# First mixer of a two-layer decoder trunk: hand-ordered loops replaced by planned strands, with halved products and three partial output sums

## The chip, the cores and the metric

The kernel runs on one core of one Trainium2 chip. The metric is device time in microseconds (us); lower is better. Engines: PE (TensorE: matrix products and transposes), PEld (its weight loads), DVE (VectorE), ACT (ScalarE), POOL (GpSimd), and SP (SyncE, which issues nearly all DMAs).

## What is computed

The reference runs two decoder layers on 256 tokens of width 1024, in float32. Each layer is a half-step feed-forward block, a mixer, and a second half-step feed-forward block, with a normalization before and after each. The change concerns the mixer of the first layer, in which two branches share one input and one output projection:

```
def nsa_ssd_mixer(h, ...):
    proj = h @ w_in
    q, kc, vc, ks, vs, kw, vw, gl, z, xbc, dt = split(proj)
    q, kc, ks, kw = rope(q) / 8, rope(kc), rope(ks), rope(kw)
    o_a = nsa_attention(...)      # per head: gated sum of three softmax attentions over 15
                                  # compressed keys (kc, vc), selected blocks (ks, vs), a window (kw, vw)
    o_b = mamba2_branch(...)      # conv over 4 tokens + silu, chunked state-space scan (2 chunks of 128),
                                  # times silu(z), then an rms norm per group of 512 channels and token
    return concatenate([o_a, o_b], -1) @ w_out
```

The compressed keys and values are `silu(blk @ w1) @ w2`, where `blk` is 32 tokens plus a learned position term `pe`. With 256 tokens every block is selected and the window covers all, so the last two attentions are causal softmaxes over all tokens.

## The kernel before, in words

**Weights.** Weights stream from HBM in units of up to 512 KB. Each unit is split into two float32r parts, `whi` (written by ACT) and `wlo` (the rest, by DVE), and a product with activations, split the same way, is three float32r products (`mm3`, L323). Raw units sit in four buffers (`raw`), split pairs in two rings: `ringa` with 4 pairs, which always exists, and `ringb` with 6, open only in some stages (`ring`, L643).

**Stages.** First feed-forward block (f10), first mixer (`mix0`, L661), second block (f20), third block (f11), second mixer (`mix1`, L1142), last block (f21). `constants` (L607), called inside f10, loads tables. The two token tiles (t = 0, 1, of 128 tokens) share each weight unit; `lagged` (L467) runs t = 1 a few units behind t = 0.

**Order of work.** In the feed-forward blocks and in `mix0` the order on each engine follows the program text, which the framework's scheduler may rearrange. While `strict` is set (`_Engine`, L101), every instruction depends on the one issued before it on its engine, so the text is the order. `mix1` is written as strands: generators that yield the engine they want next and what they wait for. `_Plan` (L145) keeps a time for every engine, prices instructions (`count`, L190), and always advances the strand whose next step can start first, counting its priority in ns as a delay (`run`, L239).

**The mixer now.** `work_a` (L752) computes q, then k and v, then the rest with m0a's 12 units; `qkv_end` (L715) applies the rotation and transposes. Then `ringb` closes and `compress` (L818), `attend_cmp` (L856), `scores` (L884), `values` (L916) and the 12 projections `do_xbc` (L792) run in a loop whose lags are written out by hand; `scores` multiplies all 128 partitions of q by keys with the other head group's rows zeroed (`kTz`), and DVE adds the mask while it takes the maximum (`pr`). Then `ringb` reopens, and a second loop (L1088) runs `decays` (L1026), the 8 gate projections `do_z` (L804), `outputs` (L1053), `gated` (L1061) and `normed` (L1075); the last scales each token by its norm through a product with a diagonal matrix (`dg`). Finally `work_o` (L1109) and `finish` (L573) form the output product with m0o's 12 units, over all 12 in one accumulation per token tile and half, then the norm and the residual. PSUM has four `acc` banks, two `fill` banks (projections, and t = 0 of the output product) and two `tp` banks (transposes).

**The parts that the change touches most.** In `compress` the bias of the hidden layer, `pe` times `w1`, is 16 products of one column per branch, on tiles `pv` and `cwp`; `values` runs all products of one output half (v) before the other's; `decays` multiplies float32 `da`, spread over 128 columns, by a triangular table, and masks the first chunk with one float32r product and the second on DVE.

## Time and profile before

| what | value |
|---|---|
| time before, median of 3 runs | 1214.81 us (1214.44 to 1224.08) |
| the profiled execution's own time | 1214.29 us |
| its span (first to last instruction) | 1212.5 us |
| PE busy | 1183.3 us (98%) |
| DVE busy | 775.7 us (64%) |
| ACT busy | 596.2 us (49%) |
| HBM read | 189.24 MB, 157 GB/s over the span |

Busy time of PE is the union of its matmul records; a record lasts longer than the step from one product to the next, since they are pipelined. The granted clock (PEclk) is given as a share of 2.4 GHz; it has two levels, 1.2 and 2.4 GHz. In this trace nearly every instruction is recorded under the helper's line L112, so groups are told apart by tile names: `fill<-xth,whi` is a product written to a `fill` bank from tiles `xth` and `whi`. A float32 product appears as two instructions, a float32r product as one.

### The profile page before, as it was taken

What the parts mean: (1) busy time and instruction counts of PE and PEld (TensorE: products, weight loads), DVE (VectorE), ACT (ScalarE), POOL (GpSimd) and SP (SyncE); (2) the same over time, 40 slices, a digit from 0 to 9 for tenths busy, and PEclk for the clock granted to TensorE, in tenths of its full rate; (3) what the DMA queues carried; (4) which work ended last, traced back from release to release, by engine and by line L of the source; (5) the groups of instructions that cost most, each with busy time, mean ns of one, the idle gap of its engine ahead of it and who ended that gap; (6) DMA issues with size and microseconds to landing.
All of it is one profiled execution on the core that took longest, in us unless ns stands there. A gap on an engine that the chain in (4) does not pass through costs nothing. (4 is left out here: it accounts for less than half of the span.)

```text
span 1212.5 us, 17861 instructions
## 1 busy us (share of the span) xinstructions
PE 1183.3 (98%) x6888; PEld 999.4 (82%) x6888; DVE 775.7 (64%) x1401; ACT 596.2 (49%) x992; POOL 15.8 (1%) x43
## 2 busy tenths in 40 slices
PE   8999999989999999999999999989999999999997
PEld 6888887878997788888888888889988887888885
DVE  6755548677697765554675564457894688755543
ACT  6655545447663564553465554256234135655531
POOL 0000000000000000000000000001100000000000
PEclk9999999889999999999999999999999999999999
DMA  8765563512163176555575555340414131755540
GB/s 302 248 200 184 189 181 94 202 53 88 49 232 121 55 261 206 191 177 193 169 235 185 188 191 188 116 168 25 154 61 156 39 121 65 264 195 189 189 158 35
DMA packets 53876, 191.46 MB, mean 158 GB/s; under 512 B 6621, under 2 KB 6621, under 8 KB 53662
## 3 DMA queue, kind: packets, MB, share of 16 engines
q1 hardware_dynamic: 53790, 190.31, 46.3%
q8 instruction: 54, 0.88, 0.3%
q14 instruction: 32, 0.26, 0.1%
HBM read 189.24 MB, written 1.05 MB: 157 GB/s over the span
## 5 line engine op out<-in xcount | busy, mean ns | idle before, releaser
L112 DVE SCALAR_TENSOR_TENSOR wlo<-raw,gch,whi 128x1024 fp32r<-128x1024 f32 (+2 forms) x214 | 237.0, 1125 | 143.9 <-ACT whi L112 143.5
L112 ACT ACTIVATE whi<-raw,gch 128x1024 fp32r<-128x1024 f32 (+2 forms) x214 | 214.0, 1023 | 152.7 <-PE acc L112 110.6
L112 DVE TENSOR_TENSOR wlo<-raw,whi 128x1024 fp32r<-128x1024 f32 x120 | 146.5, 1224 | 123.9 <-ACT whi L112 123.9
L112 PE MATMUL acc<-whi,xtl 128*128 128x512 f32 (+1 forms) x576 | 223.6, 388 | 1.1 <-DVE xtl L112 1.1
L112 PE MATMUL acc<-wlo,xth 128*128 128x512 f32 (+1 forms) x576 | 224.1, 390 | 0.0
L112 PE MATMUL acc<-whi,xth 128*128 128x512 f32 (+1 forms) x576 | 221.9, 392 | 0.3 <-DVE u L112 0.3
L112 ACT CAST whi<-raw 128x1024 fp32r<-128x1024 f32 x120 | 125.9, 1051 | 140.5 <-PE acc L112 114.1
L112 PE MATMUL acc<-whi,hth 128*128 128x512 f32 x352 | 137.6, 391 | 0.0
L112 PE MATMUL acc<-whi,htl 128*128 128x512 f32 x352 | 137.1, 389 | 0.0
L112 PE MATMUL acc<-wlo,hth 128*128 128x512 f32 x352 | 137.0, 389 | 0.0
L112 PEld LDWEIGHTS acc<-whi,xtl 128*128 128x128 f32 x576 | 108.3, 188 | 23.2 <-DVE xtl L112 1.5
L112 PEld LDWEIGHTS acc<-whi,xth 128*128 128x128 f32 x576 | 108.8, 189 | 22.0 <-DVE u L112 0.7
L112 PEld LDWEIGHTS acc<-wlo,xth 128*128 128x128 f32 x576 | 108.5, 188 | 20.9
L112 PE MATMUL acc<-whi,xt 128*128 128x512 f32 x352 | 111.0, 391 | 0.0
L112 PEld LDWEIGHTS acc<-whi,htl 128*128 128x128 f32 x352 | 66.1, 188 | 13.9
L112 PEld LDWEIGHTS acc<-whi,hth 128*128 128x128 f32 x352 | 66.1, 188 | 13.6
L112 PEld LDWEIGHTS acc<-wlo,hth 128*128 128x128 f32 x352 | 66.1, 188 | 13.5
L112 PEld LDWEIGHTS acc<-whi,xt 128*128 128x128 f32 x352 | 66.0, 188 | 13.5
L112 PE MATMUL acc<-wlo,xt 128*128 128x512 f32 x176 | 69.0, 392 | 0.0
L112 PE MATMUL fill<-xth,whi 128*128 128x256 f32 x160 | 48.2, 302 | 4.0 <-DVE c L112 3.8
L112 PE MATMUL fill<-xth,wlo 128*128 128x256 f32 x160 | 47.2, 296 | 0.0
L112 PE MATMUL fill<-xtl,whi 128*128 128x256 f32 x160 | 47.2, 295 | 0.0
(380 smaller groups left out, 1695.3 us busy)
## 6 DMA issues: line engine op xcount, KB each, us to landing
raw<-in_wst_dram SPq DMA_DIRECT2D x301, 512.0 KB, 3.5
lw<-in_wst_dram SPq DMA_DIRECT2D x12, 512.0 KB, 3.5
grow<-in_rows_dram SPq DMA_DIRECT2D x9, 512.0 KB, 4.8
wlo<-in_wst_dram SPq DMA_DIRECT2D x8, 512.0 KB, 4.8
whi<-in_wst_dram SPq DMA_DIRECT2D x8, 512.0 KB, 5.0
wr<-in_wst_dram SPq DMA_DIRECT2D x8, 512.0 KB, 11.1
lw<-in_lw_dram SPq DMA_DIRECT2D x3, 512.0 KB, 3.6
raw<-in_wst_dram SPq DMA_DIRECT2D x4, 296.0 KB, 3.1
```

Source lines behind the costliest of these rows:

```text
L112: r = f(out, *a, **k)
```

## The change

`mix0` is rewritten as strands, ordered by `_Plan` with priorities of its own, and emitted with `strict` on. The output of f10's second token tile is normalized inside the mixer (`second`). PSUM has six `acc` banks throughout. k and v are computed before q. The bias of `compress` is computed once in `constants` (`cbias`) from another load of `w1`. The two branches of `compress` alternate between output partitions 0-63 and 64-127, as do the heads in `values` and `outputs`; `scores` uses the 64 partitions of one head group each, without zeroed rows. The causal mask is added by a float32r product of the identity and a mask whose entries are 0 and 1e30 (signs are turned: scores are negated, and their minimum is taken). `decays` uses two float32r parts of `da` and a mask product for both chunks. The output product has three partial sums (attention, and the two groups of the state-space branch); the group's norm weight goes into the output weights (`split`), and the token's norm scales the partial sum (`summed`). `normed` and `dg` are gone. The projections use ring `ringa` with four pairs; `ringb` closes once both `work_a` strands are done, its place holds the mixer's tiles, and it reopens after the last output (`swap`).

```diff
-    a = [(w, 2 * h, 2, c) for c in (qc, kv, rest) for h in range(4)]
+    a = [(w, 2 * h, 2, c) for c in (kv, qc, rest) for h in range(4)]
...
+                ns = max(n / 0.6 + 5, 1.68 * m) * (0.65 if out.shape[0] <= 64 and n >= 30 else 1.0 if a[0].shape[0] > 64 else 0.55 if n > 200 else 0.8)
...
+    PRIORITY0 = {"scale": 500, "normed": 282, "work_a": 300, "end_k": 249, "end_q": -300, "end_r": -389, "split_a": 0, "split":
+                 100, "project": 300, "convolved": 204, "gate": 0, "compress": -366, "attend": 141, "scores":
+                 200, "values": 100, "steps": 213, "products0": 410, "tokens0": 163, "carry": 647, "decays":
+                 -17, "weights": 300, "outputs": 141, "gated": 195, "project_out": 497, "summed": 324,
+                 "finish": 98, "split_f": 330, "second": 200}
...
+            if kind == "mixer":
+                self.y1 = y(1)
+            else:
+                self.postnorm(1, y(1), grow_post, half)
...
+        w = self.xp.tile([P, 2, 16, 64], F32, name="cw", tag="x8")
+        nc.sync.dma_start(w, self.cw[:, 0:2048].rearrange("p (s j e) -> p s j e", s=2, e=64))
+        self.cbias = self.cp.tile([P, 1], F32, name="cbias")
+        tp = self.tpp.tile([P, 4, P], F32, name="tp", tag="tp")
+        for i in range(2):
+            nc.vector.tensor_mul(w[:, i], w[:, i], self.pvt[:, 76 + 16 * i:92 + 16 * i, None].to_broadcast([P, 16, 64]))
+            sums = self.sm.tile([P, 64], F32, name="cbs", tag="cbs", bufs=2)
+            nc.vector.tensor_reduce(sums, w[:, i].rearrange("p j e -> p e j"), axis=mybir.AxisListType.X, op=ALU.add)
+            nc.tensor.matmul(tp[64 * i:64 * i + 64, 0, 0:1], sums, self.tabt[:, 767:768], start=True, stop=True)
+        nc.vector.tensor_scalar(self.cbias, tp[:, 0, 0:1], 0.5, None, op0=ALU.mult)
...
+        def split(name, i, where):
...
+            yield "act", ev("raw", name, i), where, *([ev("ring")] if name == "f20" else [])
+            if where is sl:
+                yield "act", sl
...
+            g = self.gain(ph[name], i) if name in ("m0a", "f20") else normw[:, i - 4:i - 3, None] if name == "m0o" and i > 3 else None
+            if g is None:
+                nc.scalar.copy(hi, x)
+                yield "dve"
+                nc.vector.tensor_sub(lo, x, hi.bitcast(F32))
+            else:
+                for k in range(sh[1]):
+                    if k:
+                        yield "act"
+                    nc.scalar.activation(hi[:, k], x[:, k], AF.Copy, scale=g[:, k])
+                    yield "dve"
+                    nc.vector.scalar_tensor_tensor(lo[:, k], x[:, k], g[:, k], hi[:, k].bitcast(F32), op0=ALU.mult, op1=ALU.subtract)
...
+        def project(name, i):
+            yield "pe", pa, ev(name, i), ev("xn", 0), ev("xn", 1)
+            a = acc((S,))
+            hi, lo = us[name, i]
+            for k in range(KD):
+                self.mm3(a, hi[:, k, :], lo[:, k, :], xn[0][:, k, :], xn[1][:, k, :], k == 0, k == 7)
+                if k % 2 and k < 7:
+                    yield "pe"
+            give(ra)
...
+            ps = acc()
+            R = [slice(64 * i, 64 * i + 64) for i in range(2)]
+            for j in range(16):
+                for i in range(2):
+                    nc.tensor.matmul(ps[R[i], 0:30], w1[i][:, j, :], cst[:, 2 * i:2 * i + 2, 2 * j:2 * j + 225:16], start=j == 0, stop=j == 15)
+                if j % 4 == 3 and j < 15:
+                    yield "pe"
...
+            nc.scalar.activation(ht[:, 0, :], ps[:, 0:30], AF.Tanh, scale=0.5, bias=self.cbias)
+            nc.scalar.activation(ht[:, 1, :], ps[:, 0:30], AF.Identity, scale=0.5, bias=self.cbias)
+            yield "dve"
...
         def scores(t, g):
...
             ns = P * (t + 1)
...
+            ps = []
+            for v in range(2):
+                yield "pe", pa, ev("q", t), ev("k", 0), *([ev("k", 1)] if t else [])
+                ps.append(acc((2, ns)))
+            for v in range(2):
+                vs = slice(64 * v, 64 * v + 64)
+                nc.tensor.matmul(ps[v], qT[vs, g, TS[t]], kT[vs, :, 0:ns], start=True, stop=False)
+            for v in range(2):
+                nc.tensor.matmul(ps[v][:, :, ns - P:ns], self.identr, self.cmaskr[:, None, :].to_broadcast([P, 2, P]), start=False, stop=True)
+            drop("qT", "kv")
+            yield "dve", ql
+            sm = self.sm.tile([P, 3, 4], F32, name="s4", tag="s4")
+            for v in range(2):
+                if v:
+                    yield "dve"
+                nc.vector.tensor_reduce(sm[:, 0, 2 * v:2 * v + 2], ps[v], axis=mybir.AxisListType.X, op=ALU.min)
+                plan.spend("dve", 1.05 * ns)
             for i in range(4):
...
+                    nc.vector.tensor_copy(pT[:, 4 * h:4 * h + 4, :], tp)
+                    plan.spend("dve", 200.0)
+                give(pt)
+            yield "pe", pa, ev("pc"), ev("cmp", 1), *(ev("rest", b) for b in range(nb))
             op = acc()
+            for i, (b, blk) in enumerate([(b, blk) for b in range(2) for blk in range(nb)]):
+                for v in range(2):
+                    nc.tensor.matmul(op[64 * v:64 * v + 64, 0:P], vtok[:, blk, P * b + 64 * v:P * b + 64 * v + 64], pT[:, (2 * v + b) * nb + blk, :],
+                                     start=i == 0, stop=False)
+                if i == 1:
+                    yield "pe"
             for v in range(2):
...
                 j = 2 * g + v
...
+        def decays(c, g, hq):
...
+            h0 = 8 * g + 4 * hq
+            yield "pe", pa, ev("da")
+            ab = acc((4, P))
+            mask = lambda start, stop: nc.tensor.matmul(ab, self.identr, self.smaskr[:, None, :].to_broadcast([P, 4, P]), start=start, stop=stop,
+                                                     skip_group_check=stop)
+            if c == 0:
+                mask(True, False)
+            for i in range(4):
+                for d in (dah, dal):
+                    nc.tensor.matmul(ab[:, i, :], d[:, c, h0 + i:h0 + i + 1].to_broadcast([P, P]), self.triur,
+                                     start=c == 1 and i == 0 and d is dah, stop=i == 3 and d is dal)
+            yield "act", sl, *([] if c else [ev("dst")])
+            w = slot([2, 4, P], "seg")
+            seg, ca = w[:, 0], w[:, 1]
+            if c:
+                nc.scalar.activation(ca, ab, AF.Exp)
+                yield "pe"
+                mask(False, True)
+            for i in range(4):
+                if c or i:
+                    yield "act", ev("dst")
+                nc.scalar.activation(seg[:, i, :], ab[:, i, :], AF.Exp, bias=nacs[:, c, h0 + i:h0 + i + 1])
+            give(pa)
+            segs[c, g, hq] = seg, ca
...
+        def outputs(c, g):
+            yield "pe", pa, ev("seg", c, g, 0), ev("xd", c, g), *([ev("st", g)] if c else [])
+            yp = acc((4, P))
+            for hq in range(2):
+                if hq:
+                    yield "pe", ev("seg", c, g, 1)
+                seg, ca = segs[c, g, hq]
+                for j in range(2):
+                    if j:
+                        yield "pe"
+                    for x, w in ((xd[c], seg), (held["st"], ca))[:1 + c]:
+                        for b in range(2):
+                            h = 8 * g + 4 * hq + 2 * j + b
+                            nc.tensor.matmul(yp[64 * b:64 * b + 64, 2 * hq + j, :], x[:, 64 * h:64 * h + 64], w[:, 2 * j + b, :],
+                                             start=w is seg, stop=c == 0 or w is ca)
...
+        def gated(c, g, yp):
...
+            cs = TS[c]
+            yield "dve", ev("skip", g), sl
+            w = slot([2, 4, P], "y")
+            y, sq = w[:, 0], w[:, 1]
+            nc.vector.tensor_add(y, yp, xsT[g][:, :, cs])
+            give(pa)
...
+            yield "act", ev("yt")
+            hi, lo = [a[:, 4 * g:4 * g + 4, cs] for a in yt]
+            nc.scalar.copy(hi, y)
+            yield "dve"
+            nc.vector.tensor_sub(lo, y, hi.bitcast(F32))
+            fire("yt", c, g)
+            yield "act"
...
+            for m in range(4):
+                nc.tensor.matmul(ps[:, 0, 0:1], sq[:, m, :], one, start=m == 0, stop=m == 3)
+            give(sl)
+            yield "dve"
+            nc.vector.tensor_copy(ssq[:, c, g:g + 1], ps[:, 0, 0:1])
+            give(pt)
+            fire("ss", c, g)
+            if g:
+                yield "dve", ev("ss", c, 0)
+                rg[c] = self.rsqrt([ssq[:, c]], 2, 1.0 / 512, 4e-5)
+                fire("rg", c)
...
+        def project_out(t):
...
+            for p in range(3):
                 for h in range(2):
...
+                    hs = slice(512 * h, 512 * h + 512)
+                    for k in range(4):
+                        i = 4 * p + k
+                        yield "pe", ev("m0o", i), ev("yt", t, p - 1) if p else ev("o", t, k), *([] if k else [pa])
+                        if k == 0:
+                            ps = acc()
+                        x = [a[:, k if p == 0 else i - 4, TS[t]] for a in (yt if p else oT)]
+                        wh, wlo = us["m0o", i]
+                        self.mm3(ps, *x, wh[:, 0, hs], wlo[:, 0, hs], k == 0, k == 3)
+                        if h:
+                            drop(("m0o", i))
+                            if i >= 8:
+                                drop(("m0o", i, 1))
+                    if p == 0:
+                        e = plan.sooner("act", "dve")
+                        yield e, *([] if h else [sl])
+                        if h == 0:
+                            s[t] = slot([2, 512], "s")
+                        if e == "act":
+                            nc.scalar.copy(s[t][:, h], ps)
+                        else:
+                            nc.vector.tensor_copy(s[t][:, h], ps)
+                            plan.spend("dve", 200.0)
+                        give(pa)
+                        if h:
+                            fire("att", t)
+                    else:
+                        add(summed(t, p, h, ps), pr["summed"])
+            if t:
+                give(xl)
+                give(xl)
...
+        def summed(t, p, h, ps):
+            yield "dve", ev("rg", t), *([ev("sum", t, p - 1, h)] if p > 1 else [])
+            nc.vector.scalar_tensor_tensor(s[t][:, h], ps, rg[t][:, p - 1:p], s[t][:, h], op0=ALU.mult, op1=ALU.add)
+            give(pa)
+            fire("sum", t, p, h)
+            if p == 2:
+                fire("y", t, h)
+                if h == 0:
+                    add(finish(t), pr["finish"])
...
+        def swap():
...
+            yield "pe", ev("wa", 0), ev("wa", 1)
+            ring.close()
+            kl = late.enter_context(tc.tile_pool(name="kl", bufs=1, reuse_waits="tile"))
...
+            fire("late")
+            yield "pe", *(ev("yt", c, g) for c in range(NT) for g in range(2)), ev("att", 0), ev("att", 1)
+            late.close()
+            ring.enter_context(self.ring())
+            rb.clear()
+            for _ in range(RINGX):
+                give(rb)
+            fire("ring")
...
+        add(work_a(0), pr["work_a"])
+        add(work_a(1), pr["work_a"])
+        loads = [load("m0a", i) for i in range(LAG, 9)] + [load_row("grow", gpre)] + [load("m0a", i) for i in range(9, 12)] + [load_compress()]
+        loads += [load("m0x", i) for i in range(12)] + [load("m0z", i) for i in range(4)] + [load("m0o", i) for i in range(4)]
+        loads += [load("m0z", i) for i in range(4, 8)] + [load("m0o", i) for i in range(4, 12)] + [load_row("row", gpost)]
+        add(chain(*loads, *(load("f20", i) for i in range(AHEAD))))
+        add(chain(*(split("m0a", i, rb if 4 <= i < 10 else ra) for i in range(LAG, 12))), pr["split_a"])
+        add(chain(*(split("m0x", i, ra) for i in range(12)), *(split("m0z", i, ra) for i in range(4)),
+                  *(split("m0o", i, ra) for i in range(4)), *(split("m0z", i, ra) for i in range(4, 8)),
+                  *(split("m0o", i, ra) for i in range(4, 8)), *(split("m0o", i, sl) for i in range(8, 12))), pr["split"])
+        add(chain(*(project("m0x", i) for i in range(12)), *(project("m0z", i) for i in range(8))), pr["project"])
+        add(compress(), pr["compress"])
+        add(attend(), pr["attend"])
```

## Rows read from the trace of the kernel before

**Rows 1.** the page's busy times: busy us (share of the span) xinstructions
```profile
PE 1183.3 (98%) x6888; PEld 999.4 (82%) x6888; DVE 775.7 (64%) x1401; ACT 596.2 (49%) x992; POOL 15.8 (1%) x43
```

**Rows 2.** windows, both mixers: length, busy us (xcount), PEclk, DMA share, GB/s
```profile
196.20:412.90 216.70, 206.06 (x1421) 177.83 (x1420) 159.58 (x446) 117.54 (x269) 2.65 (x7) 0.95 0.33 112
785.70:1017.70 232.00, 227.59 (x2069) 201.96 (x2068) 170.46 (x375) 96.67 (x255) 10.29 (x22) 0.99 0.28 101
```

**Rows 3.** windows of ten us in the first mixer
```profile
240.00:250.00 10.00, 10.00 (x76) 9.49 (x74) 4.43 (x22) 1.52 (x4) 0.00 (x0) 0.63 0.00 0
260.00:270.00 10.00, 6.34 (x48) 5.66 (x47) 9.31 (x50) 7.39 (x32) 0.00 (x0) 1.00 0.11 42
```

**Rows 4.** PE's waits in the first mixer: total us, times, longest us
```profile
PE fill L112 <- DVE c L112: 3.8, 1, 3.8
```

**Rows 5.** timeline of PE, compress: start us, us, engine, line, operation, tiles
```profile
233.63 3.58 PE L112 MATMUL acc<-cst,cwp 128*64 128x30 f32 x32
237.03 2.70 PE L112 MATMUL acc<-pv,cwp 128*64 128x1 f32 x24
...
248.45 2.06 PE L112 MATMUL acc<-cst,cwp 128*64 128x30 f32 x32
250.34 2.00 PE L112 MATMUL acc<-pv,cwp 128*64 128x1 f32 x32
```

**Rows 6.** timeline of PE, two products of the scores (four instructions)
```profile
256.77 1.96 PE L112 MATMUL acc<-kTz,qT 128*128 128x512 f32 x4
258.57 0.51 PE L112 MATMUL acc<-da,tabs 128*128 128x16 f32 x4
```

**Rows 7.** timeline of PE in the second mixer, row-halved products
```profile
900.36 0.49 PE L112 MATMUL acc<-rhT,beT 64*128 64x128 f32 x4
900.68 0.39 PE L112 MATMUL acc<-kk,aT 64*128 64x128 f32 x4
900.90 0.39 PE L112 MATMUL acc<-rhT,aT 64*128 64x128 f32 x4
901.22 0.66 PE L112 MATMUL tp<-ident,aT 128*128 128x128 f32 x4
901.81 0.49 PE L112 MATMUL acc<-rhT,beT 64*128 64x128 f32 x4
```

**Rows 8.** timeline of PE, a projection at the lower, then the full clock
```profile
246.83 0.41 PE L112 MATMUL fill<-xtl,whi 128*128 128x256 f32 x1
247.04 0.41 PE L112 MATMUL fill<-xth,wlo 128*128 128x256 f32 x1
...
247.79 0.28 PE L112 MATMUL fill<-xtl,whi 128*128 128x256 f32 x1
247.91 0.28 PE L112 MATMUL fill<-xth,wlo 128*128 128x256 f32 x1
```

**Rows 9.** timeline of PE, column-halved outputs, mask and decays
```profile
343.16 0.66 PE L112 MATMUL acc<-seg,xd 128*64 128x128 f32 x8
343.75 0.49 PE L112 MATMUL acc<-smaskr,identr 128*128 128x512 f32 x1
344.08 1.05 PE L112 MATMUL acc<-tabs,da 128*128 128x128 f32 x8
345.06 0.33 PE L112 MATMUL acc<-seg,xd 128*64 128x128 f32 x2
```

**Rows 10.** timeline of PE, values at the second token tile
```profile
304.53 1.09 PE L112 MATMUL acc<-pT,vtok 128*64 128x128 f32 x8
305.45 0.38 PE L112 MATMUL acc<-pcT,vrep 128*64 128x128 f32 x2
```

**Rows 11.** groups, DVE, first mixer: xcount | busy us, mean ns | idle before
```profile
L112 DVE TENSOR_TENSOR wlo<-raw,whi 128x1024 fp32r<-128x1024 f32 x32 | 38.7, 1220 | 11.6 <-ACT whi L112 11.6
```

**Rows 12.** timeline of SP at the start
```profile
5.24 0.48 SPq L614 DMA_DIRECT2D tabs<-in_tabs_dram  x1
```

**Rows 13.** window at the start, columns as in rows 2
```profile
12.00:16.00 4.00, 4.00 (x20) 3.25 (x19) 3.89 (x12) 2.96 (x6) 0.00 (x0) 1.00 0.99 340
```

More of the change, by code (lines that the diff above doesn't have):

```diff
@@ new lines, in mix0 @@
+        for i in range(12):
+            share(("m0a", i), 2, rb if 4 <= i < 10 else ra)
+            share(("m0o", i), 2, ra if i < 8 else sl)
+            if i >= 8:
+                share(("m0o", i, 1), 2, sl)
+        pr = self.PRIORITY0
+        raw, us = {}, {("m0a", i): w for i, w in enumerate(self.ahead)}
+        for i in range(LAG):
+            ev("m0a", i).at = 0.0
+        self.ahead = []
+        qT, kv, cst = [slot([4, S], n) for n in ("qT", "kv", "cst")]
+        for _ in range(3):
+            sl.pop()
@@ new lines, in sums, with scale @@
+        def sums(t, y):
+            st = self.sm.tile([P, 2], F32, name="st", tag="st")
+            for h in range(2):
+                yield ("act", ev("y", t, h)) if y is s.get(t) else "act"
+                junk = self.cp.tile([P, 512], F32, name="junk", tag="junk", bufs=1)
+                nc.scalar.activation(junk, y[h] if isinstance(y, list) else y[:, h], AF.Square, accum_out=st[:, h:h + 1])
+            return [st[:, 0:1], st[:, 1:2]]
+        def scale(t):
+            ss = yield from sums(t, [self.xs[t][:, 512 * h:512 * h + 512] for h in range(2)])
+            yield "dve"
+            self.r[t] = self.rsqrt(ss, 1, 1.0 / D, 1e-6)
+            fire("r", t)
@@ new lines, in second @@
+        def second():
+            yield "act", ev("y1"), sl
+            u = slot([2, 512], "u")
+            ss = yield from sums(1, y1)
+            for h in range(2):
+                yield "dve"
+                nc.vector.tensor_mul(u[:, h], y1[h], self.rowsp[:, 0, 512 * h:512 * h + 512])
+                give(pa)
+            drop("rows")
+            yield from update(1, ss, u, 4.0)
+            give(sl)
+            for h in range(2):
+                yield from parts(self.xs[1][:, 512 * h:512 * h + 512], [a[:, 4 * h:4 * h + 4, TS[1]] for a in self.xt])
+            fire("xt", 1)
+            add(scale(1), pr["scale"])
+            add(normed(1), pr["normed"])
@@ L969, in mix0 @@
-        compress()
-        attend_cmp()
-        items = [(t, g) for t in range(NT) for g in range(4)]
-        probs = {}
-        for n in range(12):
-            if n < 8:
-                probs[n] = scores(*items[n])
-            if n == 1:
-                steps()
-            if 2 <= n < 10:
-                values(*items[n - 2], probs.pop(n - 2))
-            do_xbc(n)
-        sa.close()
-        sb = ExitStack()
-        ms = pool(sb, "ms", side="right")
-        t2 = lambda shape, name: ms.tile([P] + shape, F32, name=name, tag="t2", bufs=6)
@@ L996, in states, with products @@
+            give(pa)
+            yield "act"
+            nc.scalar.activation(dst, dst, AF.Exp)
+            fire("dst")
+        def products():
+            yield "pe", pa, *(ev("x", m) for m in range(8, 12))
+            ps = acc((NT, 2, P))
+            bc = xsT[2]
             for c in range(NT):
-                cs = slice(P * c, P * c + P)
                 for g in range(2):
-                    o = P * (2 * c + g)
-                    nc.tensor.matmul(ps[:, o:o + P], bcT[:, g, cs], bcT[:, 2 + g, cs], start=True, stop=True)
@@ L1119, in mix0 @@
[L1119 to L1124 removed]
+                nc.tensor.transpose(tp[:, g, :], bc[:, g, 0:P], self.ident)
+            yield "act"
+            nc.scalar.copy(held["btok"], tp[:, 0:2, :])
+            give(pt)
+            fire("btok")
@@ new lines, in mix0 @@
+        add(chain(*(project("m0x", i) for i in range(12)), *(project("m0z", i) for i in range(8))), pr["project"])
+        add(compress(), pr["compress"])
+        add(attend(), pr["attend"])
+        for t in range(NT):
+            add(chain(*(scores(t, g) for g in range(4))), pr["scores"])
+        add(steps(), pr["steps"])
+        add(products(), pr["products0"])
+        for h in range(2):
+            add(tokens(h), pr["tokens0"])
+        add(chain(*(decays(c, g, hq) for c in range(NT) for g in range(2) for hq in range(2))), pr["decays"])
```

797 lines of the change are left out of this document (438 added, 359 removed).

## Prediction

> **What bounds the kernel now.** I read the page's busy times first: TensorE (PE) is busy 98% of the span [rows 1]. That share hides differences between stages, so next come the stage windows: the first mixer runs from 196.2 to 412.9 us, with PE busy 206.06 of 216.70 us at a mean granted clock of 0.95; the second mixer, whose order a planner already writes, has 227.59 of 232.00 us at 0.99 [rows 2]. In the first mixer VectorE (DVE) is busy 159.58 us and ScalarE 117.54 us, so over the whole stretch PE is the bound, and time is won in two ways: fewer PE instructions, and fewer stalls or slow-clock stretches. Ten-microsecond windows show where the latter lie [rows 3]: from 240 to 250 us PE looks full, but the granted clock is 0.63, which is mostly the lower level of 1.2 GHz; from 260 to 270 us PE is busy 6.34 us only, while DVE is busy 9.31 us. The longest PE wait is there, 3.8 us on DVE's convolution of a projected block [rows 4]. A matmul record overlaps the next one, so prices below are distances between starts in the timeline, unless I say otherwise.
>
> **The change, part by part (PE).** In microseconds of the mixer; minus is a gain.
>
> *Bias products of compress.* The 64 instructions on `pv` leave for one precomputed `cbias`. 32 of them ran at the full clock and lasted 2.0 together; the other 32 ran at the lower clock, where the products on `cst` took 3.40 (233.63 to 237.03) instead of 1.89 (248.45 to 250.34), so some 3.5 [rows 5]: together **-5.5**.
>
> *Compress, column-halved.* 64 instructions on `cst` stay, 5.3 now [rows 5]; key and value products now alternate between output rows 0-63 and 64-127. Upper end 3.8 (64 at the full-clock price, no overlap), lower end 1.9 (perfect pairs). No row shows pairs of 30 columns; I take the middle, 2.9: **-2.4**.
>
> *Scores, row-halved.* 24 instructions of 512 columns at 1.80/4 = 0.45 [rows 6] are 10.8. Afterwards each of eight (token tile, head group) steps has two products of 64 rows. The second mixer shows such pairs: four instructions, two pairs, from 900.68 to 900.90, so a pair costs 0.11 [rows 7], what one unpaired instruction of 128 columns costs by a quarter of that 0.45. So four steps of two pairs at 0.225 and four of two pairs at 0.45 are 5.4: **-5.4**. The mask moves from DVE to PE: 16 exact float32r products of 256 columns at 0.12 [rows 8]: **+1.9**.
>
> *The price of switching halves.* From one start of halved products to the next, 900.36 to 901.81, are 1.45 us for six pairs (0.67) and four transposes (0.45): 0.33 is left for one switch in and out [rows 7]. The column-halved outputs of the first mixer give the same: 343.16 to 345.06 is 1.90; less four pairs (0.45), a 512-column mask (0.23) and eight decay products (0.90), 0.32 is left [rows 9]. Column trips exist before and after; eight row trips are new: 8 x 0.33, **+2.6**. The Trainium skill (TensorEngine Tiling (Array Packing), Key Properties) says that a change of the tiling mode, and not merely of the tile, drains TensorE. By that rule the halved scores are worth less than their doubled rate; without it the sum would be 2.6 us lower. The trace agrees, with 0.32 to 0.33 us a trip.
>
> *Values.* At the second token tile eight instructions of one half follow each other, 304.53 to 305.45, 0.115 each: no overlap [rows 10]. Alternating halves makes them 0.056: 80 x 0.059 = 4.7. The first token tile already overlaps in part; I book 0.3 for its 48. **-5.0**.
>
> *Decays.* 32 float32 products (two instructions each) become 64 float32r ones of 128 columns. No row shows a float32r product that narrow. Lower end: 128/256 of 0.12, 0.06 (3.4 won); upper end: twice the present 0.112 (7.2 lost). I take 0.112, the price of the present ones [rows 9], which have the same weights and columns: **0**. Four more masks of 512 columns: **+0.9**. The eight `dg` products of the norm leave: **-0.9**.
>
> PE sum: -5.5 - 2.4 - 5.4 + 1.9 + 2.6 - 5.0 + 0.9 - 0.9 = **-13.8**.
>
> **Stalls and clock.** Idle now: 216.70 - 206.06 = 10.6 [rows 2]. Lower clock: 0.05 x 216.7 / 0.5 = 21.7 us, in which a 256-column product takes 0.21 instead of 0.12 [rows 8], so at most 44% or 9.5 is lost; some 3.1 of that is booked above under compress, 6 stay. Pool: 16.6. The strands offer the 20 projections and the attention part of the output product as filler at any time; the row that says what such an order leaves is the second mixer [rows 2]: 4.4 idle plus 0.01 x 232 / 0.5 x 0.44 = 2.0, scaled by 191/232: 5.3. **-11.3**.
>
> What is late next is DVE. It sheds the masked maxima, the second chunk's `seg` and the norm's scaling, and gains 16 reductions and eight token scalings of 512 elements, 0.6 each by half of 1.22 [rows 11]; booked at nothing, since some 160 us lie beside 192 of PE; without that cover the scalings alone cost 4.9. ScalarE gains 12 single-head exponentials and eight skip scalings: at 0.6 each 12 us, hidden beside 117.54 of 192, 12 if not. SP loads the same units in one fixed order at a DMA share of 0.33 [rows 2]. GpSimd loses four copies.
>
> **Start of the kernel.** `constants` now also loads 1 MB for `cbias` and works on it with four DVE operations of 1,024 elements at 1.22 [rows 11], 4.9 in all. The tables of the same function are issued at 5.24 us [rows 12], and from 12 to 16 us DMA is 0.99 and DVE 3.89 of 4.00 busy [rows 13]. Ends: 0 (put later, hidden), or 1.05 MB at 340 GB/s = 3.1 plus 4.9 = 8. The DMA part is the likelier, as that window is full of weight loads; PE never idles in it, so it has some products in hand: **+2.5**.
>
> **Sum.** -13.8 - 11.3 + 2.5 = -22.6 against the profiled execution's own 1214.29 us (span 1212.5; 0.5 below the median of 1214.81): **1192 us**.
>
> **Rivals.**
> - *The stalls only move.* PE work falls, but the order waits elsewhere: the projections have four weight slots until the ring reopens, and the output units 0 to 3 hold all four until both attention sums are done. For it: DVE's 9.31 of 10 us in one window [rows 3]. Against: the second mixer's 4.4 idle. 1214.3 - 13.8 + 2.5 = 1203 us. Chance 0.18.
> - *Halved pieces get scattered.* Strands can be interrupted between pieces (compress two more pieces, values eight, outputs eight). If full products come between, 18 x 0.33 = 5.9 more: 1198 us. This is where the drain that the Trainium skill names (TensorEngine Tiling (Array Packing), Key Properties) would decide. Against: most of their priorities come ahead of the projections'. Chance 0.08.
> - *Narrow float32r products cost double.* +7.2: 1199 us. Chance 0.09.
> - *Slower: the clock.* Half-used arrays and narrow products fill more of the mixer, and the clock falls there as around the compress products [rows 3, 5]. Each microsecond at the lower level loses 0.44, so the gain is gone with 22.6/0.44 = 51 us of it, and 1227 us is reached with 80 (now 21.7, most of which the forecast already removes). Against: the second mixer has halved products and keeps 0.99 [rows 2, 7]. Chance 0.05.
> - The order is emitted as strict dependencies, so the change can hardly fail to do what it says; a gain lost to the start and to unbooked evacuations has 0.05, near no change.
>
> **Numbers.** Forecast 0.55, its own range 1184 to 1199. Range over all: the low end has narrow decays (-3.4), perfect pairs in compress (-1), a hidden start (-2.5) and stalls of 2 (-3.3), and a margin against all of these coming together and more, 1178; the high end goes past the first rival and the start's upper end, 1206. A measurement of this kernel can tell about 1% (12 us) from no change. Faster by more: forecast, scattered, narrow, and 0.08 of the first rival and the unbooked, 0.80; within 1%: what is left of these two, 0.15; slower 0.05.
>
> **What will show it.** A mixer stretch near 192 us; idle near 5 us in it; the `pv` products gone from it; score pairs at the price of one product; 0.112 between decay products; no new PE gap before 35 us. It is wrong if DVE is full for tens of microseconds in the mixer, if the clock there stays at or below 0.95, or if the first feed-forward block gets longer by over 8 us.

## The result and the profile after

The changed kernel takes 1205.8 us (median of eight runs, 1193.08 to 1213.01) beside 1215.7 us for the kernel before on the same chip: a ratio of 0.9893, 95% interval 0.9853 to 0.9933. The forecast was 1192 us with a range of 1178 to 1206, so the median lies at its upper edge. The profiled execution is the shortest of the eight, 1193.08 us with a span of 1190.8. The other seven lie between 1204 and 1213 us with a mean clock of 0.968 to 0.976, so one profile is not enough here; experiment 1 takes a second one of the same kernel. Medians in this document are those of all runs; a ratio leaves out executions that its comparison marks as disturbed.

Windows over the five stages of the changed kernel (start:end, length, busy us of each engine with its instructions, granted clock, DMA share, GB/s): the first feed-forward block, the first mixer, the two blocks between, the second mixer, the last block.

```profile
0.00:200.90 200.90, 192.49 (x864) 158.63 (x865) 122.63 (x157) 105.46 (x131) 1.60 (x9) 0.99 0.67 213
200.90:381.20 180.30, 179.89 (x1378) 157.62 (x1377) 153.58 (x337) 119.11 (x282) 0.00 (x0) 1.00 0.39 129
381.20:755.20 374.00, 372.90 (x1697) 308.15 (x1696) 222.18 (x289) 187.52 (x228) 1.01 (x6) 1.00 0.57 188
755.20:996.10 240.90, 234.08 (x2069) 208.08 (x2068) 172.21 (x375) 96.29 (x252) 10.38 (x22) 0.95 0.28 98
996.10:1183.00 186.90, 186.28 (x845) 153.47 (x843) 105.94 (x135) 90.00 (x111) 0.00 (x0) 1.00 0.53 172
```

Against [rows 2] the first mixer fell from 216.7 to 180.3 us (-36.4, where 25.1 was forecast), its PE idle time from 10.6 to 0.4, and its clock rose from 0.95 to 1.00. The second mixer, whose code the change doesn't touch, rose from 232.0 to 240.9 at a clock of 0.95. The first block ends 4.7 us later (200.9 for 196.2), the middle blocks take 374.0 for 372.8, and the last one 194.7 for 194.8 (its window above ends with TensorE's last product, not with the span). Sum: +4.7 - 36.4 + 1.2 + 8.9 - 0.1 = -21.7, which is the difference of the spans, 1212.5 to 1190.8.

Two first-mixer products after the change, in the timeline of PE: a score step and its masks, then values at the second token tile.

```profile
235.59 1.13 PE L112 MATMUL acc<-kv,qT 64*128 64x512 f32 x4
236.65 0.51 PE L112 MATMUL acc<-cmaskr,identr 128*128 128x256 f32 x2
...
260.77 1.09 PE L112 MATMUL acc<-pT,kv 128*64 128x128 f32 x16
261.70 0.39 PE L112 MATMUL acc<-pc,vrep 128*64 128x128 f32 x4
```

Sixteen value instructions now take 0.93 us (260.77 to 261.70), about what eight took in [rows 10] (0.92). Four score instructions of 64 rows take 1.06 us (235.59 to 236.65), where two pairs at the price of one full instruction each would take 0.90; the other 0.16 I put down to a change of tiling, which these rows alone don't show.

### The profile page after: what moved, and what is told of

It reads as the page before. It is cut to its first block, busy times and chain, and to the rows that moved or that the text cites. A ratio compares the mean times of both kernels' runs of the same rounds, so it can differ in the third digit from the quotient of the medians.

```text
span 1190.8 us, 17670 instructions
## 1 busy us (share of the span) xinstructions
PE 1165.6 (98%) x6848; PEld 986.0 (83%) x6848; DVE 780.0 (66%) x1302; ACT 599.1 (50%) x1002; POOL 13.0 (1%) x37
## 4 chain that ended last, share of the span: by engine, by line
PE 91%; DVE 4%; DMA 2%; issue 1%; ACT 1%; SPq 0%; DVEq 0%; ACTq 0%
PE acc L112 87%; PE tp L112 4%; DMA lw<-in_lw_dram 1%; DVE wlo L112 1%; DMA raw<-in_wst_dram 1%; DMA x<-in_x_dram 0%; DVE wl L112 0%; DVE rs_a L112 0%; DVE xu L112 0%; ACT junk L112 0%; ACT whi L112 0%; DVE tm L112 0%; DVE rs_y L112 0%; DVE x L112 0%; DVE yA L112 0%
## 5 line engine op out<-in xcount | busy, mean ns | idle before, releaser
L112 DVE TENSOR_TENSOR wlo<-raw,whi 128x1024 fp32r<-128x1024 f32 x112 | 137.1, 1224 | 116.7 <-ACT whi L112 116.4
L112 ACT CAST whi<-raw 128x1024 fp32r<-128x1024 f32 x112 | 117.7, 1051 | 124.2 <-PE acc L112 110.2
L112 PEld LDWEIGHTS acc<-whi,htl 128*128 128x128 f32 x352 | 66.1, 188 | 13.8
L112 PE MATMUL acc<-xnh,whi 128*128 128x256 f32 x160 | 46.6, 291 | 0.0
L112 PE MATMUL acc<-xnl,whi 128*128 128x256 f32 x160 | 45.2, 282 | 0.0
L112 PE MATMUL acc<-xnh,wlo 128*128 128x256 f32 x160 | 45.2, 282 | 0.0
```

The lines of the kernel that those rows point to most:

```text
L112: r = f(out, *a, **k)
```

## Experiments

Unless said otherwise, the edit stands against the changed kernel.

**1. Where the typical run loses its time** (no edit).

> The changed kernel as it is, for a second profile and as the measure of the other three. The profile so far has the second mixer at 242.1 us against 232.0 before, with 0.95 of the clock, although its code is untouched. Theory A (the planner's new count for float32 products also re-orders the second mixer, and the new order costs it): the second mixer is again 240 us or more, and what the typical run has above 1193 lies there as stretches at the lower clock. Theory B (chance of one execution): the second mixer returns to 232 and the typical run's extra time lies in the feed-forward blocks.

Measured: 1207.54 us (1192.01 to 1212.84), ratio 0.9878 (0.9832 to 0.9923). The profiled execution took 1212.84. Its windows, first and second mixer:

```profile
200.10:380.40 180.30, 179.90 (x1378) 157.63 (x1377) 153.66 (x337) 119.07 (x282) 0.00 (x0) 1.00 0.39 129
...
754.40:1015.90 261.50, 255.10 (x2069) 225.41 (x2068) 172.41 (x375) 96.30 (x252) 10.38 (x22) 0.86 0.26 90
```

The length of the first mixer repeats; all that this execution has over the first one is in the second mixer, 261.5 us at 0.86 for 240.9 at 0.95. (The 242.1 us of the expectation counts from 754.0 us, 1.2 us ahead of that window.) This is the longest of the six executions; experiment 3 shows the same stretch in a second kernel. Theory A's first half holds.

**2. The old count for the second mixer.** The class of the planner holds a `count` that prices each PE product; the change multiplied its float32 price by a factor, and the second mixer is planned with the same class.

```
-        plan = self.plan = _Plan(sp=-8000.0)        # first mixer
+        plan = self.plan = _Plan(True, sp=-8000.0)
...
-    ... * (0.65 if out.shape[0] <= 64 and n >= 30 else ...)
+    ... * (1.0 if not self.halves else 0.65 if out.shape[0] <= 64 and n >= 30 else ...)
```

> The changed kernel with the new count for float32 products used only while the first mixer is planned; the second mixer is planned with the old count, so its order is that of before. Theory A: the second mixer is back at 232 us and 0.99 of the clock, 10 us less than in the profile of the changed kernel, and the whole stands 10 to 20 us under the changed kernel's median, at 1185 to 1195. Theory B: within 3 us of the changed kernel. Theory C (the second mixer's loss comes from where the first mixer now leaves tiles in SBUF): the second mixer stays at 240 or more.

Measured: 1183.73 us (1181.87 to 1184.76), ratio 0.9723 (0.9704 to 0.9741); clock 0.997. The second mixer:

```profile
755.00:986.80 231.80, 227.57 (x2069) 201.97 (x2068) 170.46 (x375) 96.75 (x255) 10.29 (x22) 0.99 0.29 102
```

It is back at the 232.0 us of [rows 2], and the whole is some 24 us under experiment 1's median, more than the 10 to 20 expected. TensorE's products in the stage come in the same order as in the kernel before, record by record. Theories B and C fall.

**3. The new count in the kernel before, and nothing else.**

```
-                ns = max(n / 0.6 + 5, 1.68 * m)
+                ns = max(n / 0.6 + 5, 1.68 * m) * (0.65 if out.shape[0] <= 64 and n >= 30 else 1.0 if a[0].shape[0] > 64 else 0.55 if n > 200 else 0.8)
```

> The kernel before with the new count for float32 products and nothing else: only the order of the second mixer changes. Theory A: slower than before by 10 to 20 us, 1225 to 1235, with the second mixer at 240 us or more and a lower clock in it; everything else as before. Theory B and Theory C: no change, 1213 to 1217.

Measured: 1241.48 us (1230.10 to 1245.09) beside 1216.6, ratio 1.0167 (1.0131 to 1.0203): +25 us by the medians, +20 by the ratio, at or above the upper end of the 10 to 20 expected. The second mixer:

```profile
787.70:1048.50 260.80, 255.09 (x2070) 225.35 (x2069) 172.40 (x375) 96.31 (x252) 10.37 (x22) 0.86 0.26 90
```

One line of pricing makes a kernel without the new first mixer slower, by the same stretch at the same clock, and TensorE's products there come in the order of experiment 1 (but for one record that only one of the two traces has).

**4. The bias sums held back.**

```
-    {1: second, 24: self.constants}
+    {1: second, 24: lambda: self.constants(hth[1].bitcast(F32)[:, 0, 0:1])}
...
+        nc.vector.tensor_copy(w[:, 0, 0, 0:1], late)
         nc.sync.dma_start(w, self.cw[:, 0:2048]...)
```

> The changed kernel with the load and the sums of the compression's bias held back until the second hidden tile of the first feed-forward block exists (one more DVE copy of one column). If these operations are what moves the first mixer's start from 196.2 to 200.9, the first product of the mixer comes at 196 to 197 and the whole is 4 to 5 us under the changed kernel. If the 4.7 us come from something else in the first 30 us (the shorter table load, the new copies of masks), the start stays at 200 to 201 and the time does not move.

Measured: 1189.11 us (1187.62 to 1193.42), ratio 0.9772 (0.9752 to 0.9792). The place is right, the size needs care: the start of the mixer is counted from a span start that differs by a microsecond or two between executions. Counted from the first 512-column product of the kernel (8.28 us before, 8.71 after, 9.39 in experiment 1, 9.94 here) to the first product of the mixer it is 187.9 us before, 192.2 after, 190.7 in experiment 1 and 188.7 here. (Experiment 3, whose first block is that of before, has 188.7, so the count is good to about 1 us.) The bias costs 2.0 us by experiment 1; the profile after paid 1.5 more for a stretch at the lower clock. The whole is 18 us under experiment 1's median, where 4 to 5 were expected. The remaining 16 us must lie behind the start. The one profile here has the second mixer at 239.6 us, like the first profile after, although PE's order there is nearly that of the changed kernel:

```profile
750.60:990.20 239.60, 234.07 (x2070) 208.02 (x2069) 170.90 (x375) 94.43 (x249) 10.64 (x23) 0.95 0.29 101
```

The five runs lie within 6 us of each other, so the 261.5 us of experiment 1 is in none of them. Why this order meets the lower clock less often here stays open; with the old count nothing of it is left (next).

**5. Both together.**

> The changed kernel with the old count for the second mixer and the bias sums held back, together. The other runs of this call are edits of this one. If the two parts are independent (the bias costs 2.0 us at the start: 190.7 against 188.7 us from the first 512-column product to the first mixer product): 1181 to 1182, clock 0.997. If the 18 us that holding back the bias gave by itself were more than its 2 us and a luckier second mixer: 1175 or less.

Measured: 1182.00 us (1179.68 to 1183.87), ratio 0.9720 (0.9690 to 0.9749), as expected of independent parts. Counted as in experiment 4, the first mixer starts at 188.8 us (190.7 in experiment 2), and the second mixer keeps its old length. The 1.7 us between this median and experiment 2's would not show by itself: the ratios are 0.9720 and 0.9723. First and second mixer:

```profile
198.10:378.30 180.20, 179.80 (x1377) 157.58 (x1376) 153.45 (x337) 118.96 (x282) 0.00 (x0) 1.00 0.38 128
...
752.60:985.20 232.60, 228.65 (x2069) 203.06 (x2068) 170.33 (x375) 96.77 (x255) 10.29 (x22) 0.99 0.29 101
```

This version beats the kernel before and the changed kernel. It is the base of experiments 6 to 11, which call it "both".

**6. Halves of the columns one after the other.** In `compress` and `values` the loops over halves and over pieces change places:

```
-            for j in range(16):
-                for i in range(2):
+            for i in range(2):
+                for j in range(16):
```

> As both, but the column halves of the compression and of the values are issued one half after the other in place of alternately; number, shape and operands of the products are the same. If alternate halves overlap, as the 28 ns from one to the next of a pair suggests, undoing it costs the forecast's 2.4 and 5.0 us: both + 7. If the gain came from the smaller shape alone, no change.

Measured: 1187.07 us (1186.47 to 1191.34), ratio 0.9771 (0.9743 to 0.9800): both + 5.1. The first mixer:

```profile
198.90:384.30 185.40, 185.16 (x1377) 163.04 (x1376) 153.97 (x337) 119.23 (x282) 0.00 (x0) 1.00 0.37 125
```

PE busy rises by 5.36 us with the same instructions and no idle time: alternate halves do overlap. (In the profile after, the two products of a compress pair start 7 ns apart and the next pair 51 or 52 ns later; the 28 ns of the expectation is about half of that step.) It is less than 7.4: one-sided compress costs 3.8 us end to end at the full clock and not the 5.3 of [rows 5], part of which ran at the lower one (+1.7 for 2.4), and the values take 3.8 more for 5.0. End to end means here and below: each product is counted from the end of the one before it to its own, waits included.

**7. Scores over full rows.** `qT[vs, g, TS[t]], kT[vs, :, 0:ns]` becomes `qT[:, g, TS[t]], kT[:, :, 0:ns]`.

> As both, but the products of the scores run over all 128 rows (both heads' rows at once, so the scores are sums over two heads and the output is not the reference's). Forecast's terms: the halves gave -5.4 us and their changes of tiling cost 2.6, so undoing both costs +2.8: 1184 to 1185. If the change of tiling costs nothing: +5.4, 1187. If it costs as much as the halves give, or the product is hidden beside other work: within 1 us of both.

Measured: 1200.87 us (1198.03 to 1205.53), ratio 0.9881 (0.9850 to 0.9912): both + 19, outside everything expected. PE's products of scores and masks took 3.3 us more end to end, but the planner prices full rows differently, so the whole mixer was emitted in another order: it takes 192.8 us in place of 180.2, with TensorE waiting 3.0 us for DVE's `s` and 2.6 us for ScalarE, and the blocks behind it 379.5 in place of 374.3, with 3.8 us for a late `wlo`.

**8. The same, order held.** The products run over full rows while the planner is told of halves.

```
+                self.plan = None
                 nc.tensor.matmul(ps[v], qT[:, g, TS[t]], kT[:, :, 0:ns], start=True, stop=False)
+                self.plan = plan
+                plan.count("pe", "matmul", ps[v], (qT[vs, g, TS[t]], kT[vs, :, 0:ns]), {})
```

> The full-row scores once more (sums over two heads, so the output is not the reference's), but the planner counts them as the halves, so every engine keeps the order of the kernel named both (1182.0 us). In full_rows the products of scores and masks together took 3.3 us more end to end (11.42 + 2.08 against 6.77 + 3.48), the whole 19 us more, and the order had changed too. If the other 15 us were the order: both + 3 to 4 us, 1185 to 1186. If the wider products themselves delay the exponentials and bring the waits: 1195 or more.

Measured: 1185.05 us (1181.70 to 1188.88), ratio 0.9749 (0.9725 to 0.9772): both + 3.0. The first mixer:

```profile
197.80:380.30 182.50, 182.09 (x1378) 161.08 (x1376) 153.79 (x337) 119.33 (x282) 0.00 (x0) 1.00 0.38 127
```

PE busy is 2.29 us above both. So halving the rows gives 2 to 3 us net of its switches, and the other 16 us of experiment 7 came with the order. The Trainium skill (TensorEngine Tiling (Array Packing), Key Properties) says that a change of the tiling mode drains TensorE. The runs agree in size: twice the rate on the forecast's 10.8 us would be 5.4 us, less eight trips at 0.33 it would be 2.8, and 2.3 us of PE time was measured.

**9. The projections first.** The same instructions; in `PRIORITY0`, `"project": 300` becomes `"project": -20000`.

> As both, but the 20 projection strands of the first mixer go ahead of everything else in the planner (their priority from 300 to -20000), so the dense work is used up early; all instructions are the same. If the 18 us of idle time and low clock that left the first mixer went because the planner keeps dense products beside the attention's waits: PE idle 8 us or more again in the mixer, lower clock there, and 10 to 25 us more than both. If they went because there are fewer and shorter instructions: within 3 us.

Measured: 1206.98 us (1204.70 to 1208.08), ratio 0.9924 (0.9896 to 0.9951): both + 25. The first mixer, whole and in three of its ten-us windows, then PE's longest waits there (total us, times, longest):

```profile
197.70:398.10 200.40, 187.60 (x1370) 160.45 (x1368) 150.91 (x334) 117.26 (x278) 0.00 (x0) 0.97 0.33 113
...
260.00:270.00 10.00, 8.19 (x56) 7.71 (x55) 8.30 (x18) 5.92 (x11) 0.00 (x0) 0.83 0.47 166
...
300.00:310.00 10.00, 7.35 (x41) 4.25 (x41) 9.14 (x38) 7.12 (x29) 0.00 (x0) 0.96 0.00 0
310.00:320.00 10.00, 8.97 (x70) 7.57 (x70) 6.66 (x20) 6.47 (x23) 0.00 (x0) 0.70 0.00 0
```

```profile
PE acc L112 <- DVE wlo L112: 2.8, 5, 0.8
PE tp L112 <- DVE xd L112: 2.8, 1, 2.8
PE tp L112 <- DVE x L112: 1.6, 1, 1.6
```

Idle is 12.8 us again and the lower clock is back, as in [rows 2, 3]. The mixer takes 20.2 us more than in both, the blocks behind it 5.9 more. From 300 to 340 us no projection stands beside the attention, where DVE is busy 9.14 of 10 us at first, and 4.7 of the idle time lies there. The rest lies elsewhere: 3.3 us from 250 to 270 us, where projections do run, and most of the other 4.8 behind 340 us, where a fifth of the projections come after all and wait for their own splits. So it was the order that held the idle time down. That it did so by keeping projections beside the attention is shown for a part of that time only.

**10 and 11. Which part of the count costs the second mixer.** The factor of experiment 3 has clauses; each run gives the second mixer some of them.

```
10: * (1.0 if not self.halves and not (out.shape[0] <= 64 and n >= 30) else 0.65 if ...)
11: * (1.0 if not self.halves and out.shape[0] <= 64 and n >= 30 else 0.65 if ...)
```

> As both, but the second mixer is planned with one part of the new count: products with at most 64 output partitions and at least 30 columns (its 32- and 64-row pieces of the inverses) at 0.65. If the second mixer loses its clock because these pieces look cheap to the planner: at least 15 us of the 25 come back, 1197 or more, with 20 us or more of the second mixer at the lower clock. If it is the other part of the count: within 4 us of both.

> As both, but the second mixer is planned with the other part of the new count alone (0.55 for over 200 columns with at most 64 rows, 0.8 for the other products with at most 64 rows). The counterpart of price_small: within 4 us of both if the small pieces are the cause; 1197 or more if not. If either part alone costs it, the old order was simply the better one of many, and neither price is the cause by itself.

Measured: price_small 1190.92 us (1177.93 to 1192.97), ratio 0.9776 (0.9739 to 0.9813); price_rest 1179.80 us (1178.39 to 1187.38), ratio 0.9720 (0.9694 to 0.9747). Their second mixers, in that order:

```profile
751.10:994.10 243.00, 238.72 (x2070) 210.98 (x2069) 170.80 (x375) 96.70 (x255) 10.29 (x22) 0.93 0.28 97
```

```profile
752.70:983.20 230.50, 225.35 (x2069) 202.51 (x2068) 170.98 (x375) 96.15 (x252) 10.23 (x22) 0.99 0.29 102
```

The price of the small pieces alone costs 8.9 us over both by the medians (6.8 by the ratios), the rest alone nothing. That meets neither number of the expectation: it is more than 4 us and less than 15. The 15 us that I asked for came from runs without the bias held back; with it, the whole new count costs 1189.1 - 1182.0 = 7.1 (experiment 4), and the small pieces' price accounts for that. Why the same count costs 24 us without the hold-back they don't tell. One of the six executions of price_small took 1177.93 us at a mean clock of 0.997, so even this order can run without the loss.

**12. Light work kept further apart.** The new count everywhere, with the bias held back; compare experiment 4.

```
-        add(chain(*(grams(q) for q in range(4))), pr["grams"], 4000)
+        add(chain(*(grams(q) for q in range(4))), pr["grams"], 16000)
...
-            add(invert(q), pr["invert"], 8000)
+            add(invert(q), pr["invert"], 32000)
```

> The changed kernel with the bias held back and the new count everywhere, but the planner's penalty on light work in the second mixer (grams and inverses put off while the engine's recent work is light) four times as high: 16000 and 32000 for 4000 and 8000. If the lower clock comes from light pieces standing too close together, spreading them brings the second mixer back to 232 to 236 us and the whole to 1182 to 1186. If the new order loses for another reason (a late load, a late split), the second mixer stays at 239 or more and the whole at 1188 or more.

Measured: 1182.44 us (1181.04 to 1183.56), ratio 0.9725 (0.9707 to 0.9744). The second mixer:

```profile
751.00:984.00 233.00, 227.49 (x2069) 201.93 (x2068) 170.97 (x375) 95.67 (x252) 10.22 (x22) 0.99 0.29 101
```

With the same prices, a stronger penalty on light work brings the stage back from 239.6 us, and the whole 6.7 us under experiment 4.

**How the second mixer loses its clock.** Windows of the same code in the old order (experiment 2), then in the new one (experiment 1):

```profile
868.00:878.00 10.00, 9.84 (x140) 7.80 (x139) 9.85 (x19) 6.61 (x37) 0.00 (x0) 1.00 0.33 122
878.00:888.00 10.00, 10.00 (x162) 8.18 (x161) 8.89 (x25) 5.44 (x10) 0.96 (x1) 1.00 0.54 161
888.00:898.00 10.00, 10.00 (x190) 8.62 (x187) 1.51 (x4) 3.38 (x9) 0.00 (x0) 1.00 0.60 183
```

```profile
868.00:878.00 10.00, 10.00 (x67) 8.58 (x66) 8.84 (x19) 7.03 (x38) 0.00 (x0) 1.00 0.29 107
878.00:888.00 10.00, 8.10 (x93) 6.08 (x90) 6.14 (x13) 4.14 (x10) 0.00 (x0) 0.64 0.51 159
888.00:898.00 10.00, 10.00 (x134) 8.03 (x133) 5.85 (x14) 2.62 (x6) 1.11 (x1) 0.67 0.34 107
898.00:908.00 10.00, 10.00 (x130) 8.72 (x129) 2.58 (x7) 3.49 (x9) 0.00 (x0) 0.50 0.17 54
908.00:918.00 10.00, 10.00 (x102) 8.38 (x101) 0.42 (x1) 2.46 (x5) 0.00 (x0) 0.50 0.31 105
```

The new order starts the inverses, products of 32 and 64 rows, some ten us later (882.57 for 872.00 us), and then piles them up. PE's timeline in experiment 1, where the clock goes to the lower level at 880.9, back at 891.1, and down again at 894.5 for 34 us (three more lower stretches of the stage, of 6.8, 6.8 and 13.7 us, lie outside these windows):

```profile
880.47 0.50 PE L112 MATMUL acc<-wlo,mix 128*128 128x512 f32 x1 [1.90 <-DVE wlo L112]
...
890.99 1.19 PE L112 MATMUL acc<-xw,LT 64*64 64x64 f32 x16
892.11 1.09 PE L112 MATMUL acc<-tm,LT 32*32 32x32 f32 x32
893.13 1.14 PE L112 MATMUL acc<-LT,xw 64*64 64x64 f32 x16
...
900.74 1.97 PE L112 MATMUL acc<-xw,LT 64*64 64x64 f32 x16
902.64 1.56 PE L112 MATMUL acc<-tm,LT 32*32 32x32 f32 x29
```

The fall at 880.9 follows a wait of 1.90 us; the one at 894.5 follows 3.2 us of pieces of 32 and 64 rows, with PE 10.00 of 10 us busy and no wait. The Trainium skill (TensorE: Matmul & The Clock Gate, section "HAM oscillation — how this bites in real kernels") puts a falling clock down to the engine's waits, there for a DMA, between groups of products. In this case a wait is neither enough nor needed.

It is not enough. Experiment 11 has a wait as long on the same kind of split, just ahead of its inverses (its waits from 860 to 960 us come first below), and keeps 0.99 over the stage. The profile after has experiment 1's order of products, record by record, and the same wait, and then 16.9 us at the full clock (second and third line):

```profile
PE acc L112 <- DVE wlo L112: 1.9, 1, 1.9
...
878.20 0.50 PE L112 MATMUL acc<-wlo,mix 128*128 128x512 f32 x1 [1.91 <-DVE wlo L112]
...
878.20:895.10 16.90, 16.90 (x341) 14.24 (x341) 11.72 (x29) 7.17 (x16) 1.11 (x1) 1.00 0.48 160
```

It is not needed. In price_small (experiment 10) the only wait of PE that the profile lists from 770 to 920 us is one of 0.2 us, and the clock falls at 885.0 for 30.7 us, among its inverses:

```profile
PE tp L112 <- ACT sq L112: 0.2, 1, 0.2
...
875.00:885.00 10.00, 10.00 (x165) 8.16 (x164) 6.94 (x20) 5.15 (x17) 0.00 (x0) 1.00 0.48 156
885.00:895.00 10.00, 10.00 (x88) 8.11 (x89) 4.19 (x8) 3.06 (x8) 0.96 (x1) 0.50 0.34 109
```

Nor does a row of small pieces always bring it: experiment 2 runs 3.1 us of them from 887.11 us at the full clock. What the runs show is that the order decides how much the clock costs, and that the longest lower stretch of each profile with a loss begins among these pieces. What it takes for the clock to fall stays open.

The price agrees with the forecast's 44%: at 0.86 of 261.5 us, 73 us run at the lower level (0.14 x 261.5 / 0.5), in the old order's profile 3.4 us; 70 x 0.44 = 31 against 261.5 - 231.8 = 29.7 measured. For the typical run, whose mean clock is 0.974 beside 0.997 in experiment 2: 0.023 x 1204 / 0.5 x 0.44 = 24 us, and the medians differ by 22 to 24.

## Why the prediction came out as it did

The median is inside the range, 14 us above the forecast; the gain of 9.9 us by the medians (13 by the ratio) is about half of the 22.6 forecast. That it lies inside is luck: two errors of opposite sign cancel in part. The first mixer won 11 us more than forecast, and a stage that I booked at nothing lost 9 us in the profile after, 30 in experiment 1's profile, and 22 to 24 in the typical execution.

**PE sum, -13.8.** Summed end to end over the groups of the stretch, before to after: bias products 5.3 to 0 (forecast -5.5); compress 5.5 to 2.15 (-3.3 for -2.4: perfect pairs, the lower end); scores, masks and switches together 11.4 to 10.2 (-1.1 for -0.9); values 13.7 to 8.5 (-5.2 for -5.0); decays 7.9 to 6.7 (-1.2 for 0: the new ones start 0.11 us apart, so 0.112 is right; the old ones ran at the full clock too, from 325 to 365 us, and the -1.2 stays unexplained); the further masks +1.5 for +0.9; `dg` -1.1 for -0.9. Together -15.7. Not priced: the outputs, whose halves alternate now as well, 7.6 to 5.85. With the next term these make some 34 of the 36.4 us; the rest is assigned to no term.

**Stalls and clock, -11.3.** Mis-sized. I left 5.3 us by the rate of the second mixer; what is left is 0.4 idle and no lower clock, so the whole pool of 16.6 went. Experiment 9 shows that the order holds it: with the same instructions in another order 12.8 us of idle time and the lower clock return. The rival "the stalls only move" needed only other priorities.

**Start, +2.5.** Right in size, 2.8 us in experiment 1 and 4.3 in the profile after, but by the other mechanism: I called the transfer the likelier part, and what PE waits for is DVE. The sign "no new PE gap before 35 us" was wrong. PE waits 2.5 us (1.6 in experiment 1) on DVE's splits behind the bias work; waits of PE up to 60 us in the profile after, and DVE's timeline there:

```profile
PE acc L112 <- DVE wlo L112: 2.5, 1, 2.5
```

```profile
20.15 2.35 DVE L112 TENSOR_TENSOR cw<-cw,pv 128x1024 f32<-128x1024 f32 x2
22.49 3.85 DVE L112 TENSOR_REDUCE cbs<-cw 128x64 f32<-128x1024 f32 x2
26.26 2.47 DVE L112 SCALAR_TENSOR_TENSOR wlo<-raw,gch,whi 128x1024 fp32r<-128x1024 f32 x2
```

The four operations take 6.2 us; I had 4.9, because I priced a reduction like a product, at 1.22 us where it takes 1.9.

**The step that failed: the second mixer is no term of the sum.** The diff shows the factor in `count`, and the prediction gives it no term. The same class plans the second mixer, so the factor gave that stage another order. Experiments 2 and 3 show it from both sides, +20 to 25 us alone and -24 us when taken back. The rival "slower: the clock" had the mechanism and its price of 0.44 per us, but put it in the first mixer, and took the second one's 0.99 as an argument against it; that 0.99 was a property of its order: with the new count the stage has 0.95 and 0.86.

**DVE and ScalarE** stayed covered as booked: 153.58 and 119.11 us beside 180.3.

## What to carry to other kernels

A planner's prices are shared state: where a diff changes one, list every stage that is planned with it, and re-time each. To measure one edit in a planned kernel, hold the order (experiment 8 against 7: 3 us and 19 us for the same products). Read the granted clock beside the busy time: among the pieces of 32 and 64 rows the clock fell to the lower level while PE read as full (experiment 10, from 885.0 us), and a plan that spreads them further took the loss away (experiment 12).

## What was not expected of the hardware

- The clock of one fixed order is not one number: the changed kernel ran at 1192 to 1196 us and at 1204 to 1213 us, with mean clocks of 0.983 to 0.988 and 0.968 to 0.976, while experiment 2's four runs stayed within 3 us.
- Two alternating column halves of 30 columns cost little more than one: 64 compress products took 2.15 us alternating and 3.8 us one side after the other.
- The same wait of 1.9 us stood ahead of a fall of the clock in one execution (experiment 1, 880.9 us) and not in another of the same order (the profile after, 878.20 us), nor in experiment 11; and in price_small the clock fell without a wait. What decides was not settled.
